# Gate and up products of an FFN by blocks: seven products of half blocks in place of eight, with the residual kept in memory

## The chip, the cores and the metric

The kernel runs on one core of a Trainium2 chip. Its time is the device time of one execution in microseconds (us). The engines are TensorE (PE, with its weight loads shown as PEld), VectorE (DVE), ScalarE (ACT), GpSimd (POOL) and SyncE (SP), which issues the DMAs.

## What is computed

Two layers, each of an FFN, a mixing sublayer and a second FFN, on x of 512 tokens by 1024 features in float32:

```
def swiglu_ffn(h, w_gu, w_down):
    a, b = jnp.split(h @ w_gu, 2, axis=-1)
    return (jax.nn.silu(a) * b) @ w_down

for l in range(DEPTH):                       # DEPTH = 2, D_FF = 2816
    h = swiglu_ffn(rmsnorm(x, ffn1_pre_g[l]), ffn1_w_gu[l], ffn1_w_down[l])
    x = x + 0.5 * rmsnorm(h, ffn1_post_g[l])
    h = mixing_sublayer(rmsnorm(x, mix_pre_g[l]), w_in[l], ...)
    x = x + rmsnorm(h, mix_post_g[l])
    h = swiglu_ffn(rmsnorm(x, ffn2_pre_g[l]), ffn2_w_gu[l], ffn2_w_down[l])
    x = x + 0.5 * rmsnorm(h, ffn2_post_g[l])
```

rmsnorm divides by the root mean square over the 1024 features and multiplies by a gain. The mixing sublayer has four branches (a gated MLP over tokens, a pooling, an attention over selected keys, a convolution of 31 taps), whose gated sum goes through w_out.

## The kernel before

Activations lie as [feature in its block of 128, block k of 8, token of 512]. Every float32 product is made of three products of halves: a rounded copy (made by ACT) and the rest (value minus copy, made by DVE or POOL). `split` does it for activations (L218 ACT, L219 DVE, or L221 and L222 with a scale), `weights` for a weight tile: a DMA of up to 512 KB into `raw` (two buffers), the copy wH on ACT (L195), the rest wL on DVE (L200, 1024 wide) or on POOL (two of 512). `mm3s` writes the matmuls (L251); each has 128 x 128 weights of its own and 512 token columns, or 256 where a sublayer's border is taken by halves of the tokens.

An FFN has 22 blocks f of 128 hidden features. For each, gate and up are products over the 8 blocks k of x: 2 x 8 x 3 = 48 matmuls of 512 columns. The operands are x times a gain per feature (xH, xL); the norm's factor by token is only applied to the results: in `gu_evac` DVE multiplies the gate product by rb_ (L453), ACT takes silu (L454), DVE multiplies with the up product (L456), and `split` makes the halves. silu is taken of the scaled gate; the scale of the up product is left to the norm behind the sublayer (`rc_prev` in `post_stats`). After each of three groups of f (GROUPS) the down product over these f is made for the 8 blocks d of the output and added up in y (L526, L528). The last four d of the last group are the tail: they are made by halves of the tokens, and the first products of the next sublayer (`head`, and `ahead` for the FFN's f = 2) lie around the norms between the two, so that PE has work while these run. The residual x stays in SBUF all the time (tiles x0 to x7).

Each engine runs its queue in the order in which the program was laid down. The chain in front of rb_ is: column sums on PE (L291), the reciprocal root on DVE in small steps (L335, L275 to L280), four diagonals (L299), their spread over the partitions on PE (L307), and ACT's copy to rb_ (L338).

Of the kernel before, what the change touches and what calls it, by code (L numbers as in the profile page):

```python
# [11 lines left out]
F32 = mybir.dt.float32  # L12
# [13 lines left out]
GROUPS = ((0, 8), (8, 15), (15, 22))  # L26
# [22 lines left out]
class Builder:  # L49
# [22 lines left out]
    def ring(self, dt=F32R):  # L72
        return self.t([P, N], dt, "h", 20)
# [41 lines left out]
    def late_consts(self):  # L115
# [7 lines left out]
        # bias of the last 256 keys of a query block: T[q, h, j] = rel_bias[bucket(q - j + 128), h]  # L123
# [5 lines left out]
        oh = self.t([P, 1024], F32, "raw", 2)  # L129
# [26 lines left out]
    def pump(self, ns):  # L156
        """emit background steps worth ns of VectorE; a step that must let products pass waits for the next call"""
# [886 lines left out]
```

## Time and profile before

| | us |
|---|---|
| median of 3 runs (2386.17 to 2389.53) | 2388.51 |
| span of the profiled execution | 2384.7 |
| PE busy | 2310.4 (97%) |
| DVE busy | 1298.2 (54%) |
| ACT busy | 820.3 (34%) |
| POOL busy | 470.8 (20%) |

The span runs from the first to the last instruction of the profiled execution; the median of the runs lies 3.8 us above it. Busy shares are means over stages that differ: in the bodies of the four FFNs, some 1220 us together, PE has no gap, DVE is busy two fifths of the time and POOL hardly at all.

### The profile page before, as it was taken

The page shows a single profiled execution, that of the slowest core. Times are in us where ns is not written, and L with a number is a line of the kernel's source. Part 1 is how long each engine was busy: PE and PEld are TensorE (multiplying, and loading weights), DVE is VectorE, ACT ScalarE, POOL GpSimd, SP SyncE. Part 2 cuts the span into 40 slices and gives each one's busy share as a digit, 9 for nine tenths or more (in the row PEclk, how much of TensorE's full clock was granted, in tenths as well). Part 3 has the DMA queues.
Part 4 walks back from the last instruction along what each step waited for, and adds up shares of the span by engine and source line. Part 5 has one row for each costly group of instructions (what it writes and reads, how often), then busy time and mean ns, then how long its engine had stood idle before and what let it go on. Part 6 is the DMA issues. An engine that isn't in the chain of part 4 may idle for free.

```text
span 2384.7 us, 28413 instructions
## 1 busy us (share of the span) xinstructions
PE 2310.4 (97%) x11158; PEld 1931.8 (81%) x11158; DVE 1298.2 (54%) x2246; ACT 820.3 (34%) x1267; POOL 470.8 (20%) x413
## 2 busy tenths in 40 slices
PE   8999998989999999999999999989899999999997
PEld 7888888767888888888888888887778888888886
DVE  5333347899734652334573333488996346524345
ACT  4232233443443432222342222344434334322221
POOL 0000003533555300000210000035445543000001
PEclk9999999999999999999999999999999999999999
DMA  5333331222223233333323333312123222332332
GB/s 167 97 105 89 111 91 61 82 65 81 83 85 98 89 91 95 96 98 95 91 80 93 108 89 105 92 60 80 62 80 98 81 90 69 107 97 94 101 93 67
DMA packets 64271, 215.69 MB, mean 90 GB/s; under 512 B 7396, under 2 KB 11144, under 8 KB 64136
## 3 DMA queue, kind: packets, MB, share of 16 engines
q1 hardware_dynamic: 64136, 213.87, 29.5%
q8 instruction: 87, 1.43, 0.3%
q14 instruction: 48, 0.39, 0.1%
HBM read 211.74 MB, written 2.10 MB: 90 GB/s over the span
## 4 chain that ended last, share of the span: by engine, by line
PE 85%; DVE 11%; issue 1%; POOL 1%; ACT 1%; DMA 0%; SPq 0%; POOLq 0%; ACTq 0%; DVEq 0%
PE mm L251 51%; PE at L251 32%; DVE ca L841 3%; DVE x L385 1%; DVE xL L396 1%; DVE t L382 1%; PE st L307 1%; DVE sc L911 1%; DVE m L910 1%; PE st L291 0%; POOL t L759 0%; DVE s L278 0%; PE at L945 0%; DVE s L280 0%; POOL wL L200 0%
## 5 line engine op out<-in xcount | busy, mean ns | idle before, releaser
L195 ACT ACTIVATE wH<-raw 128x1024 fp32r<-128x1024 f32 (+1 forms) x394 | 408.8, 1040 | 1064.6 <-issue 574.7
L251 PE MATMUL mm<-xH,wH 128*128 128x512 f32 (+1 forms) x1504 | 572.5, 390 | 8.8 <-DVE t L732 4.4
L251 PE MATMUL mm<-xH,wL 128*128 128x512 f32 (+1 forms) x1504 | 565.2, 386 | 0.0
L200 DVE TENSOR_TENSOR wL<-raw,wH 128x1024 fp32r<-128x1024 f32 (+1 forms) x292 | 349.4, 1198 | 238.8 <-ACT wH L195 238.5
L251 PE MATMUL mm<-h,wH 128*128 128x512 f32 (+1 forms) x1496 | 407.9, 353 | 0.1
L251 PE MATMUL mm<-xL,wH 128*128 128x512 f32 (+1 forms) x1504 | 393.1, 379 | 0.0
L200 POOL TENSOR_TENSOR wL<-raw,wH 128x512 fp32r<-128x512 f32 x204 | 290.3, 1446 | 351.1 <-ACT wH L195 303.8
L251 PEld LDWEIGHTS mm<-xH,wH 128*128 128x128 f32 x1504 | 284.1, 193 | 69.1 <-DVE t L732 4.9
L251 PEld LDWEIGHTS mm<-xH,wL 128*128 128x128 f32 x1504 | 284.2, 193 | 53.9 <-issue 0.9
L251 PEld LDWEIGHTS mm<-xL,wH 128*128 128x128 f32 x1504 | 278.4, 189 | 53.1
L251 PE MATMUL at<-xH,wH 128*128 128x512 f32 (+1 forms) x784 | 301.0, 385 | 7.5 <-ACT xH L221 7.4
L251 PE MATMUL at<-xH,wL 128*128 128x512 f32 (+1 forms) x784 | 297.6, 381 | 0.0
L251 PEld LDWEIGHTS mm<-h,wH 128*128 128x128 f32 x1496 | 263.2, 188 | 41.7 <-DVE t L732 0.6
L251 PE MATMUL mm<-h,wL 128*128 128x512 f32 (+1 forms) x748 | 253.8, 354 | 0.0
L251 PE MATMUL at<-h,wH 128*128 128x512 f32 (+1 forms) x776 | 219.6, 366 | 0.0
L251 PE MATMUL at<-xL,wH 128*128 128x512 f32 (+1 forms) x784 | 210.6, 378 | 0.0
L251 PEld LDWEIGHTS at<-xH,wH 128*128 128x128 f32 x784 | 149.3, 190 | 38.0 <-ACT xH L221 7.7
L189 POOL TENSOR_TENSOR h<-raw,h 128x512 fp32r<-128x512 f32 x10 | 15.1, 1534 | 807.6 <-DVE wL L200 758.3
L251 PEld LDWEIGHTS at<-xH,wL 128*128 128x128 f32 x784 | 149.0, 190 | 29.2 <-issue 1.4
L251 PEld LDWEIGHTS at<-xL,wH 128*128 128x128 f32 x784 | 147.5, 188 | 27.5
L251 PEld LDWEIGHTS at<-h,wH 128*128 128x128 f32 x776 | 140.4, 188 | 24.6
L251 PEld LDWEIGHTS mm<-h,wL 128*128 128x128 f32 x748 | 140.4, 188 | 20.4
(196 smaller groups left out, 2185.2 us busy)
## 6 DMA issues: line engine op xcount, KB each, us to landing
raw<-in_ffn_w_gu_dram SPq DMA_DIRECT2D x173, 512.0 KB, 3.6
raw<-in_w_in_dram SPq DMA_DIRECT2D x98, 512.0 KB, 3.6
raw<-in_ffn_w_down_dram SPq DMA_DIRECT2D x64, 448.0 KB, 3.4
raw<-in_ffn_w_down_dram SPq DMA_DIRECT2D x32, 512.0 KB, 3.6
raw<-in_w_branch_dram SPq DMA_DIRECT2D x16, 512.0 KB, 3.7
raw<-in_w_out_dram SPq DMA_DIRECT2D x16, 512.0 KB, 3.6
x<-in_x_dram SPq DMA_DIRECT2D x8, 256.0 KB, 6.4
out_dram<-x SPq DMA_DIRECT2D x16, 128.0 KB, 1.8
```

The source lines that it names most:

```text
L189: nc.gpsimd.tensor_tensor(lo, r, h.bitcast(F32), op=ALU.subtract)
L195: self.pin(nc.scalar.activation(h[:, :n], raw[:, :n], AF.Copy))
L200: self.pin(e.tensor_tensor(lo[:, c], raw[:, c], h.bitcast(F32)[:, c], op=ALU.subtract))
L251: self.nc.tensor.matmul(out, w[a], m[b], start=(first and i == 0), stop=(last and i == 3 * n - 1))
L307: self.nc.tensor.matmul(ps[:, s], self.ones, dg[:, s], start=True, stop=True)
L382: nc.vector.scalar_tensor_tensor(u[:, c], s.o[k][:, c], self.v(s.post[0], s.post[1] + k), pb[:, c], op0=ALU.mult, op1=ALU.mult)
L385: e.tensor_tensor(self.xt[k][:, c], self.xt[k][:, c], u[:, c], op=ALU.add)
L396: nc.vector.scalar_tensor_tensor(self.xl[k][:, c], self.xt[k][:, c], g, self.xh[k].bitcast(F32)[:, c], op0=ALU.mult, op1=ALU.subtract)
L841: nc.vector.scalar_tensor_tensor(a, hp[:, t:t + N], dw(t), a, op0=ALU.mult, op1=ALU.add)
L910: nc.vector.max(m8, sc[:, :W])
L911: nc.vector.match_replace(out=sc[:, :W], in_to_replace=m8, in_values=sc[:, :W], imm_value=GONE)
```

## The change

Of the 22 blocks f of an FFN, the first four (PLAIN) stay as they are. The other 18 are taken in nine pairs. For a pair, the weights form a 2 x 2 scheme of blocks (gate or up by the lower or upper half of the 1024 input features), and x one too (half of the features by half of the tokens, 256). A plain product of such schemes needs eight products of half blocks; the change makes it with seven, in the form of Winograd, at the price of sums of blocks before and after. Each of the seven is 2 (blocks f) x 4 (k) x 3 = 24 matmuls of 256 columns.

- `operands` makes the right sides once per FFN: x is multiplied in place by gain and rb_ (L511), then come the halves of its quarters (L520, L521) and of four sums of quarters (L530 to L533, POOL and DVE).
- `blocks` loads four weight tiles per pair, and makes four sums of them (L551, two on DVE, two on POOL) and the halves of the seven left sides (L556 ACT, L557 DVE), each two products ahead of its use.
- `units` sets the order of the products (1, 2, 6, 5, 7, 4, 3, with the next pair's 1 and 2 ahead of this pair's 4 and 3), adds the results up (ACT L632, DVE L635 to L645), takes silu and the product, and `leave` makes the halves for the down product.
- `fill` puts the finished part of the first down product (d = 0) in front of the last pair's products 4 and 3.
- As x is destroyed by `operands`, it is written to memory at the border (`x_away`) and read back when the tail's weights are loaded (`x_back`).
- The up product now carries rb_ as well, so `gu_evac` has one more multiply on POOL (L462), and `post_stats` no longer needs the factor of the norm before.
- GROUPS changes; raw has seven buffers, and one ring of 49 tiles takes in the residual and many tiles of the mixing sublayer; the convolution runs without a padded copy.

The core of the diff:

```
-GROUPS = ((0, 8), (8, 15), (15, 22))
+GROUPS = ((0, 6), (6, 14), (14, 22))
+PLAIN = 4
...
+    def x_back(self):
+        src = self.a["x"] if self.xs is None else self.xs
+        self.xt = [self.ring(F32) for _ in range(KD)]
+        for k in range(KD):
+            self.nc.sync.dma_start(self.xt[k], src[:, k, :])
...
         a1 = b.tmp()
         nc.vector.tensor_tensor(a1, pa, b.rb_, op=ALU.mult)
         nc.scalar.activation(a1, a1, AF.Silu)
+        nc.gpsimd.tensor_tensor(a1, a1, b.rb_, op=ALU.mult)
         hp = b.tmp()
         nc.vector.tensor_tensor(hp, pb, a1, op=ALU.mult)
...
+    def operands(self):
...
+        for k in range(KD):
+            nc.vector.scalar_tensor_tensor(b.xt[k], b.xt[k], b.v(self.pre[0], self.pre[1] + k), b.rb_,
+                                           op0=ALU.mult, op1=ALU.mult)
...
+        def halves(parts):
+            h, l = b.ring(), b.ring()
+            for i, src in enumerate(parts):
+                w = src.shape[-1]
+                d = slice(i * w, (i + 1) * w)
+                nc.scalar.activation(h[:, d], src, AF.Copy)
+                nc.vector.tensor_tensor(l[:, d], src, h.bitcast(F32)[:, d], op=ALU.subtract)
+            return [(h[:, c], l[:, c]) for c in (lo, hi)]
+        for p in range(H):
+            op[1][p], op[2][p] = halves([b.xt[p][:, lo], b.xt[p + H][:, lo]])
+        yield
+        for p in range(H):
+            b11, b12, b21, b22 = b.xt[p][:, lo], b.xt[p][:, hi], b.xt[p + H][:, lo], b.xt[p + H][:, hi]
+            s13, s24 = b.tmp(), b.tmp()
+            nc.gpsimd.tensor_tensor(s13[:, lo], b12, b11, op=ALU.subtract)
+            nc.vector.tensor_tensor(s24[:, lo], b22, s13[:, lo], op=ALU.subtract)
+            nc.gpsimd.tensor_tensor(s13[:, hi], b22, b12, op=ALU.subtract)
+            nc.gpsimd.tensor_tensor(s24[:, hi], b21, s24[:, lo], op=ALU.subtract)
+            op[6][p], op[4][p] = halves([s24])
+            op[5][p], op[7][p] = halves([s13])
...
+        def one():
+            r = halves(a11)
+            tt(nc.vector, S1, a21, a22, ALU.add)
+            return r
+        def two():
+            r = halves(a12)
+            tt(nc.gpsimd, a21, a11, a21, ALU.subtract)
+            tt(nc.vector, a11, S1, a11, ALU.subtract)
+            return r
+        def six():
+            r = halves(a11)
+            tt(nc.gpsimd, a12, a12, a11, ALU.subtract)
+            return r
+        return {1: one, 2: two, 6: six, 5: lambda: halves(S1), 7: lambda: halves(a21), 4: lambda: halves(a22),
+                3: lambda: halves(a12)}
...
+    def product(self, i, out, w, fresh):
+        for c in range(2):
+            o = out[:, c * 256:(c + 1) * 256]
+            todo = []
+            for p in range(KD // 2):
+                ws = slice(c * N + p * P, c * N + (p + 1) * P)
+                h, l = self.op[i][p]
+                todo += [(w[0][:, ws], h), (w[1][:, ws], h), (w[0][:, ws], l)]
...
+        order = [(f, i) for f in fs for i in (1, 2, 6, 5, 7, 4, 3)]
+        for n in range(len(fs) - 1):
+            at = 7 * n + 5
+            order[at:at + 4] = order[at + 2:at + 4] + order[at:at + 2]
...
+            if i in (1, 6, 7):
+                s[f"t{i}"] = b.tmp()
+                nc.scalar.activation(s[f"t{i}"], bank, AF.Copy)
+            if i == 2:
+                g = s["g0"] = s["t1"]
+                nc.vector.tensor_tensor(g, bank, g, op=ALU.add)
+                nc.scalar.activation(g, g, AF.Silu)
+            if i == 7:
+                nc.vector.tensor_tensor(s["t7"], s["Z"], s["t7"], op=ALU.add)
+            if i == 4:
+                nc.vector.tensor_tensor(s["g0"], bank, s["g0"], op=ALU.mult)
+                out[f] = [(b.ring(), b.ring()) for _ in range(2)]
+                self.leave(out[f], s["g0"], 0)
+            if i == 3:
+                g = s["t6"]
+                nc.vector.tensor_tensor(g, bank, g, op=ALU.add)
+                nc.scalar.activation(g, g, AF.Silu)
+                nc.gpsimd.tensor_tensor(g, g, s["t7"], op=ALU.mult)
+                self.leave(out[f], g, 1)
```

Three places show what now stands in the queues. All are in the second FFN of the first layer. On VectorE of the kernel before, behind the chain to rb_ (the L299 diagonals), there come the weights' lower halves (wL) and, for each f, three steps on products that lie in PSUM (at, mm) or on their result (h):

```order
L299 TENSOR_SCALAR t_9636<-ident,rc_9615 128x128 x4
L351 TENSOR_TENSOR s_2223_11871<-rc_9615 128x2
L200 TENSOR_TENSOR wL_9736<-raw_9733,wH_9735 128x1024
L453 TENSOR_TENSOR t_9700<-at_9286,rb__1841_9616 128x512
L200 TENSOR_TENSOR wL_9801<-raw_9798,wH_9800 128x1024
L456 TENSOR_TENSOR t_9703<-at_9287,t_9700 128x512
L453 TENSOR_TENSOR t_9709<-mm_9288,rb__1841_9616 128x512
L219 TENSOR_TENSOR h_9706<-t_9703,h_9705 128x512
```

Now, some 30 instructions behind the same diagonals, the operands' sums (L531, of t tiles that POOL writes) and lower halves (L521) stand in the same queue; h_11868 is the last one that product 6 needs, h_11872 the last one of product 5:

```order
L531 TENSOR_TENSOR t_11862<-h_10919,t_11861 128x256
L521 TENSOR_TENSOR h_11830<-t_11819,h_11829 128x512
L460 TENSOR_TENSOR t_11887<-at_11749,rb__2026_11611 128x512
L521 TENSOR_TENSOR h_11840<-t_11834,h_11839 128x512
L557 TENSOR_TENSOR wL_11981<-raw_11899,wH_11980 128x1024
L521 TENSOR_TENSOR h_11844<-t_11833,h_11843 128x512
L464 TENSOR_TENSOR t_11891<-at_11750,t_11887 128x512
L521 TENSOR_TENSOR h_11854<-t_11848,h_11853 128x512
L635 TENSOR_TENSOR t_11947<-mm_11953,t_11947 128x512
L521 TENSOR_TENSOR h_11858<-t_11847,h_11857 128x512
L557 TENSOR_TENSOR wL_12011<-raw_11903,wH_12010 128x1024
L521 TENSOR_TENSOR h_11868<-t_11862,h_11867 128x512
```

So the queue that had a few steps per f behind rb_ now has the whole making of the operands between rb_ and products 6 and 5.

On GpSimd the kernel before has nothing between the last residual sums of the border (L385) and the end of that FFN but one mask for the next layer's use (L585):

```order
L385 TENSOR_TENSOR x_62<-x_62,t_9425 128x256
L385 TENSOR_TENSOR x_64<-x_64,t_9449 128x256
L385 TENSOR_TENSOR x_66<-x_66,t_9473 128x256
L385 TENSOR_TENSOR x_68<-x_68,t_9485 128x256
L585 AFFINE_SELECT raw_10346<-raw_10346 128x512
```

After the change the same queue has these instead, in this order: a weight sum, multiplies by rb_ (L462), a second weight sum, and twelve sums of x's quarters:

```order
L390 TENSOR_TENSOR h_10919<-h_10919,t_11479 128x256
L551 TENSOR_TENSOR raw_11899<-raw_11897,raw_11899 128x1024
L462 TENSOR_TENSOR t_11695<-t_11695,rb__2026_11611 128x512
L462 TENSOR_TENSOR t_11799<-t_11799,rb__2026_11611 128x512
L551 TENSOR_TENSOR raw_11901<-raw_11901,raw_11897 128x1024
L462 TENSOR_TENSOR t_11809<-t_11809,rb__2026_11611 128x512
L530 TENSOR_TENSOR t_11819<-h_10912 128x256
L532 TENSOR_TENSOR t_11819<-h_10916,h_10912 128x256
L530 TENSOR_TENSOR t_11833<-h_10913 128x256
L532 TENSOR_TENSOR t_11833<-h_10917,h_10913 128x256
L530 TENSOR_TENSOR t_11847<-h_10914 128x256
L533 TENSOR_TENSOR t_11820<-h_10916,t_11820 128x256
```

The sums stand behind the second and third multiply, each of which waits for a silu.

On PE the kernel before goes straight on with matmuls of 512 columns, one f behind the other:

```order
L251 MATMUL at_9642<-xH_9196,wL_9646 128x512
L251 MATMUL at_9642<-xH_9197,wH_9645 128x512
L251 MATMUL at_9642<-xH_9197,wL_9646 128x512
L251 MATMUL at_9642<-xH_9198,wH_9645 128x512
L251 MATMUL at_9642<-xH_9198,wL_9646 128x512
```

Now product 2 (mm_11953) is followed by products 5 (mm_12014) and 6 (mm_11922), which alternate as their operands (h) are written; the stretch shown lies 14 matmuls behind the end of product 2:

```order
L594 MATMUL mm_11922<-h_11854,wH_11917 128x256
L594 MATMUL mm_12014<-h_11857,wH_11949 128x256
L594 MATMUL mm_12014<-h_11857,wL_11950 128x256
L594 MATMUL mm_11922<-h_11867,wH_11917 128x256
L594 MATMUL mm_11922<-h_11867,wL_11918 128x256
L594 MATMUL mm_12014<-h_11858,wH_11949 128x256
L594 MATMUL mm_12014<-h_11871,wH_11949 128x256
L594 MATMUL mm_11922<-h_11868,wH_11917 128x256
L594 MATMUL mm_11922<-h_11825,wH_11917 128x256
```

So PE's first products of a pair stand directly behind the operands' last halves, with no other product between.

## Rows read from the trace of the kernel before

**Rows 1.** The page's head, the busy shares, and the chain's shares by engine.
```profile
span 2384.7 us, 28413 instructions
...
PE 2310.4 (97%) x11158; PEld 1931.8 (81%) x11158; DVE 1298.2 (54%) x2246; ACT 820.3 (34%) x1267; POOL 470.8 (20%) x413
...
PE 85%; DVE 11%; issue 1%; POOL 1%; ACT 1%; DMA 0%; SPq 0%; POOLq 0%; ACTq 0%; DVEq 0%
```
**Rows 2.** Busy time by stretch: an FFN, a border, another FFN.
```profile
core 0: us, PE busy (x) PEld busy (x) DVE busy (x) ACT busy (x) POOL busy (x), PEclk, DMA share, GB/s
...
39.80:346.30 306.50, 306.50 (x1344) 251.54 (x1343) 119.14 (x135) 90.51 (x116) 1.13 (x3) 1.00 0.33 98
346.30:430.00 83.70, 77.71 (x510) 70.59 (x509) 64.92 (x140) 35.80 (x67) 28.96 (x27) 0.98 0.26 76
852.30:1156.20 303.90, 303.90 (x1338) 250.83 (x1337) 118.77 (x133) 88.54 (x113) 0.00 (x0) 1.00 0.32 98
```
**Rows 3.** Chain in order of time: start, us, what (512-column matmuls).
```profile
204.01 16.32 PE at L251 x72
```
**Rows 4.** Timeline, PE, 256-column matmuls of a tail: start, us, what.
```profile
355.89 0.28 PE L251 MATMUL mm<-h,wL 128*128 128x256 f32 x1
...
357.07 0.28 PE L251 MATMUL mm<-h,wL 128*128 128x256 f32 x1
```
**Rows 5.** Timeline, PE, DVE and ACT, from the column sums to rb_.
```profile
844.47 0.95 PE L291 MATMUL st<-ones,t 128*128 128x1 f32 x8
...
846.34 1.22 DVE L200 TENSOR_TENSOR wL<-raw,wH 128x1024 fp32r<-128x1024 f32 x1
...
847.56 1.22 DVE L200 TENSOR_TENSOR wL<-raw,wH 128x1024 fp32r<-128x1024 f32 x1
...
851.31 1.02 PE L307 MATMUL st<-t,ones 128*128 128x512 f32 x2
...
852.36 0.60 ACT L338 ACTIVATE rb__1337_6876<-st 128x512 f32<-128x512 f32 x1
```
**Rows 6.** Groups by line and shape: count, busy us, mean ns, idle before.
```profile
L200 DVE TENSOR_TENSOR wL<-raw,wH 128x1024 fp32r<-128x1024 f32 x228 | 279.5, 1227 | 217.8 <-ACT wH L195 217.5
L219 DVE TENSOR_TENSOR h<-t,h 128x512 fp32r<-128x512 f32 x106 | 74.8, 707 | 3.6 <-ACT h L218 2.8
L222 DVE SCALAR_TENSOR_TENSOR xL<-x,vec,xH 128x512 fp32r<-128x512 f32 x8 | 5.6, 746 | 0.0
L437 DVE TENSOR_TENSOR t<-t,t 128x256 f32<-128x256 f32 x65 | 28.1, 432 | 22.6 <-ACT t L435 19.8
L528 DVE TENSOR_TENSOR y<-mm,y 128x512 f32<-128x512 f32 x28 | 19.4, 691 | 61.7 <-PE mm L251 61.7
L744 POOL TENSOR_TENSOR y<-y,t 128x512 f32<-128x512 f32 x32 | 41.4, 1295 | 40.3 <-DVE t L742 35.8 <-DVE s L864 4.5
L437 POOL TENSOR_TENSOR t<-t,t 128x256 f32<-128x256 f32 x53 | 41.2, 778 | 403.7 <-ACT t L435 401.4
L526 ACT ACTIVATE y<-at 128x512 f32<-128x512 f32 x16 | 9.6, 597 | 59.9 <-PE at L251 59.9
L454 ACT ACTIVATE t<-t 128x512 f32<-128x512 f32 x88 | 54.3, 617 | 0.1
L307 PEld LDWEIGHTS st<-t,ones 128*128 128x128 f32 x44 | 7.4, 199 | 20.0 <-DVE t L299 16.1 <-issue 3.5
```
**Rows 7.** Timeline, DVE, one operation behind the other in an FFN.
```profile
1229.31 1.23 DVE L200 TENSOR_TENSOR wL<-raw,wH 128x1024 fp32r<-128x1024 f32 x1 [1.50 <-ACT wH L195]
1230.45 0.69 DVE L453 TENSOR_TENSOR t<-at,rb__1841_9616 128x512 f32<-128x512 f32 x1
...
1233.90 0.69 DVE L219 TENSOR_TENSOR h<-t,h 128x512 fp32r<-128x512 f32 x1
1234.51 0.68 DVE L456 TENSOR_TENSOR t<-mm,t 128x512 f32<-128x512 f32 x1
```
**Rows 8.** Timeline, DVE, seven 256-wide operations while POOL is idle.
```profile
400.68 2.85 DVE L396 SCALAR_TENSOR_TENSOR xL<-x,vec,xH 128x256 fp32r<-128x256 f32 x7
```
**Rows 9.** Timeline, the same line of DVE beside operations of POOL.
```profile
819.48 4.38 DVE L396 SCALAR_TENSOR_TENSOR xL<-x,vec,xH 128x256 fp32r<-128x256 f32 x6
...
820.22 5.87 POOL L437 TENSOR_TENSOR t<-t,t 128x256 f32<-128x256 f32 x7 [1.62 <-ACT t L435]
```
**Rows 10.** Busy time and granted clock (PEclk) in three stretches of a border.
```profile
378.00:384.20 6.20, 4.09 (x32) 3.66 (x31) 6.20 (x14) 4.34 (x9) 4.13 (x4) 1.00 0.37 103
384.20:387.60 3.40, 3.40 (x18) 3.40 (x18) 3.40 (x7) 3.40 (x10) 2.60 (x4) 0.50 0.30 120
```
**Rows 11.** DMA issues: tile, operation, count, KB each, us to landing.
```profile
raw<-in_ffn_w_gu_dram SPq DMA_DIRECT2D x173, 512.0 KB, 3.6
...
x<-in_x_dram SPq DMA_DIRECT2D x8, 256.0 KB, 6.4
```

More of the change, by code (lines that the diff above doesn't have):

```diff
@@ L86, in consts @@
         nc, sb, a = self.nc, self.sb, self.a
-        self.xt = [sb.tile([P, N], F32, name=f"x{k}") for k in range(KD)]
+        self.xs = None
         self.vec = sb.tile([P, DEPTH * NV], F32, name="vec")
@@ L315, in new_x @@
     def new_x(self):
[L316 to L317 removed]
+        self.xh = [self.ring() for _ in range(KD)]
+        self.xl = [self.ring() for _ in range(KD)]
     @property
@@ L390, in post_steps @@
                 nc.scalar.activation(self.xh[k][:, c], self.xt[k][:, c], AF.Copy, scale=g)
+                if not first:
+                    self.x_away(k)
             yield 600
@@ new lines, in product @@
+    def product(self, i, out, w, fresh):
+        b = self.b
+        for c in range(2):
[5 more added lines that the diff above has]
+                todo += [(w[0][:, ws], h), (w[1][:, ws], h), (w[0][:, ws], l)]
+            for n, (x, m) in enumerate(todo):
+                b.run_due()
+                b.pe += 118
+                b.nc.tensor.matmul(o, x, m, start=(fresh and c == 0 and n == 0), stop=(n == len(todo) - 1),
+                                   skip_group_check=True)
@@ L503, in rest @@
             nxt = b.subs[min(b.subs.index(self) + 1, len(b.subs) - 1)]
-            if gi == 1 and isinstance(nxt, Mix):
-                nxt.params()
+            last = gi == len(GROUPS) - 1
             hm = []
-            for f in range(f0, f1):
-                if f < 3:
-                    pa, pb = self.hp[f]
-                else:
+            if gi == 0:
+                hm.append(self.gu_evac(*self.hp[0]))
+                ops = self.operands()
+                next(ops)
+                for f in range(3, PLAIN):
                     wa, wb = self.gu_weights(f)
@@ L514, in rest, with fill @@
                     b.gemm(pb, wb, b.xm)
-                hm.append(self.gu_evac(pa, pb))
+                    self.hp.append([pa, pb])
+                hm.append(self.gu_evac(*self.hp[1]))
+                hm.append(self.gu_evac(*self.hp[2]))
+                for _ in ops:
+                    pass
+                for f in range(3, PLAIN):
+                    hm.append(self.gu_evac(*self.hp[f]))
+            part = []
+            def fill(done):
+                done = hm + done
+                w, p = self.dn_weights(0, f0, f1), b.cyc()
+                b.mm3(p, b.pairs(w, done, FULL), True, False)
+                part.extend([w, p, len(done)])
+            hm = hm + self.units(range(max(f0, PLAIN), f1, 2), fill)
+            if last and isinstance(nxt, Mix):
+                nxt.params()
             self.hm, self.g = hm, (f0, f1)
-            last = gi == len(GROUPS) - 1
             if last:
@@ L533, in tail_weights @@
         b = self.b
+        b.x_back()
         ds = range(KD - TAIL, KD)
```

149 lines of the change are left out of this document (103 added, 46 removed).

## The prediction, made before the result was known

> **What bounds the kernel now.** I began with busy shares and the chain [rows 1]: TensorE (PE) is busy 97% of 2384.7 us and carries 85% of the chain, VectorE (DVE) 11%. Then the stretches [rows 2]: in the body of an FFN PE is busy all of 303.9 us (1338 matmuls, 0.227 us each) while DVE is busy 119 us, ScalarE (ACT) 89 and GpSimd (POOL) nothing; the idle time of PE lies at the borders between sublayers (77.7 of 83.7 us in one). So in an FFN the count of matmul columns sets the time, DVE has 60% to spare, and whoever takes columns away and loads the vector engines instead wins only as long as these stay hidden.
>
> **The gain on PE.** By the program, 3504 matmuls of 512 columns go and 6144 of 256 columns come (36 pairs of f, each 96 of 512 replaced by 168 of 256; 48 more become halves since the tail's group now has eight f's). A 512-column step is 16.32/72 = 0.2267 us [rows 3]; 256-column steps stand (357.07−355.89)/10 = 0.118 us apart, each with weights of its own [rows 4]. Gain: 3504 × 0.2267 − 6144 × 0.118 = 794.4 − 725.0 = 69, or 71 with the 0.2271 of the whole stretch; the last digit of the ten short steps leaves 6 to either side. I take **70**. Seven eighths of the columns are worth only 9% since the short step costs 52% of the long one.
>
> The Trainium skill (TensorE: Matmul & The Clock Gate, Back-to-back issue gap) gives an isolated gap of N/2.4 + 2.5 ns, so 216 and 109 ns; by that the gain would be an estimated 85 us. The trace differs by its own spacings above, which decide.
>
> **What the vector engines do in its place, per FFN.** (a) The operands of the seven products, once the factor rb_ is known; (b) the steady pairs; (c) the ends of groups; (d) the norm chain before rb_.
>
> Durations: two operands in SBUF on DVE, 1024 wide 1.22 us, 512 wide 0.71 (with a vector factor 0.75), 256 wide 0.43; from PSUM 0.69; on POOL 512 wide 1.30, 256 wide 0.78; ACT copy 0.60, silu 0.62 [rows 6]. In a row each begins some 0.08 us before the last ends: 1.14 after the 1024-wide op, 0.61 after a 512-wide one [rows 7], 0.40 for 256 wide with a factor [rows 8]. I use these spacings: 1.14, 0.60, 0.66 (with factor), 0.34; from PSUM 0.61 to 0.65, taken 0.65; POOL 1.25 and 0.70. A 1024-wide POOL op isn't in the trace: from 256 to 512 columns POOL's op grows by 0.52 us, so 2.3 (1.30 + 2 × 0.52) is my estimate, between 1.25 and 2.6.
>
> DVE and POOL get in each other's way. Alone, seven 256-wide DVE ops take 2.85 us [rows 8]. Beside POOL ops, six of the same line take 4.38 us (0.73 each), and seven POOL ops 5.87 (0.84 each) [rows 9]. Alone the thirteen would take 6 × 0.40 + 7 × 0.70 = 7.3 us; together they took 826.09 − 819.48 = 6.6. Almost nothing overlaps: 0.9 of the sum. DVE ops that read PSUM keep their 0.69 [rows 6], so these can lie beside POOL.
>
> The Trainium skill (SBUF — State Buffer, SBUF: two separate sides) says why: a DVE op with two SBUF inputs and a GpSimd op that reads SBUF lock one port pair for a whole instruction. The 4.38 and 5.87 us agree at 256 columns; no run here shows a 1024-wide POOL op.
>
> **(a) Operands**, counted from T0, when rb_ is there (ACT's 852.36 + 0.60 in the second FFN [rows 5]). From the spread at 851.31 [rows 5] PE still has 64 products of 512 (14.5 us) and reaches product 1 at T0 + 13.2; products 1 and 2 (48 × 0.118 = 5.7) last to 18.9; products 5 and 6 could end at 24.5. DVE's queue from T0: L460 0.65, two scalings, then L464, which must wait for silu (0.62) and POOL's new multiply (1.25): done at 4.2. Six more scalings (4.0), L232 (0.6), six of L521 (2.0): 10.8. L460, L557 and two L521 end at 13.3, just in time for product 1. POOL stood still, as its second multiply (in order, ahead of all sums) waits for that L460 and its silu: it starts at 12.1. From there POOL has 1.25 + 2.3 + 1.25 + 12 × 0.70 = 13.2 us of work. DVE's ops with two SBUF inputs until the last half that products 6 and 5 need: 2 × 0.34 + 4 × 1.14 + 2 × 0.6 + 4 × 0.34 + 8 × 0.6 = 12.6. Behind one another 25.8, at 0.9 of it 23.2: ready at 12.1 + 23.2 = 35.3. If nothing overlaps and DVE's six PSUM ops (3.9) stand in line as well: 41.8. I take the middle, 38.5. Behind the last half 27 of the 48 matmuls are left (3.2 us; the order has 6, 9, 2, 2, 2 ahead of it). PE stands 38.5 + 3.2 − 24.5 = 17.2 us per FFN (14.0 to 20.5). In the first FFN PE has 1.6 us more to do. Sum 4 × 17.2 − 1.6 = **67** (54 to 80).
>
> Such waits cost clock: at one border, behind 6.2 us in which PE worked only 4.1, it had 3.4 us at 0.50 of the clock (1.2 for 2.4 GHz) [rows 10], worth 1.7 us. Four times 2 us: **8** (7 to 14).
>
> **(b) Steady pairs.** PE needs 168 × 0.118 = 19.8 us per pair (before 21.8). DVE: seven lower halves and two sums, 9 × 1.14 = 10.3, two of 256 0.7, four PSUM ops 2.6. POOL: two sums 4.6, one multiply 1.25, two of 256 1.4: 7.3. Port work 10.3 + 0.7 + 7.3 = 18.3 us, at 0.9 of it 16.5; all in line with the PSUM ops 20.9. That is 83 to 105% of PE's time, where before DVE had 39%. The 24 passages from pair to pair should cost 0 to 1.5 us each, 0.4 by the lower end: **10** (0 to 36). The 512 KB loads (3.6 us to landing [rows 11]) are as many bytes as before and start early enough (98 GB/s in these stretches [rows 2], now a tenth more).
>
> **(c) Ends of groups.** Before product 3's results reach the down product, L645 0.65, silu 0.62, POOL 1.30, ACT's and DVE's halves some 0.8 pass: 3.4 to 3.9 us. In front of them stand 12 matmuls of d=1, 2.7 us. Before, this edge cost under 0.5 us. 12 ends × 0.7: **8** (0 to 25).
>
> **(d) Norm chain.** Between PE's column sums (844.47) and the spread, DVE had two 1024-wide ops in the chain [rows 5]; now four, and POOL's a21 beside them: 2.3 us longer. The spread now stands some seven matmuls (1.6 us) later. Three FFNs × 1: **3** (0 to 9).
>
> Beside these, the residual's 40 loads and 40 writes (256 KB each; x took 6.4 us to land [rows 11]) lie in stretches where DMA is a quarter to a third busy [rows 2] and are loaded a tail ahead of their use: 0 (−5 to +10, the shorter norm after the FFN and the longer tail being the minus).
>
> **Sum:** −70 + 67 + 8 + 10 + 8 + 3 = +26. Span 2384.7 + 26 = 2410.7; the median stands 3.8 above the span (2388.5 against 2384.7), so **2414.5 us**, 1.1% slower. The saved columns are spent while PE waits for the operands they need.
>
> **Rivals.** *Operands hidden, faster.* If DVE and POOL do not exclude each other here (other widths, other ops than in rows 9), the halves are ready when DVE's own 12.6 + 3.9 us are done: 12.1 + 16.5 = 28.6, stall 7.3 per FFN, in all 28, clock 7, pairs and ends 10: −70 + 45 = −25, 2364 us. It decides from a stall of about 11 us per FFN downwards. For it: DVE's 60% idle time. Against: rows 8 and 9.
> *Balance.* All at their low ends, 54 + 7 + 9: −70 + 70 = 0, 2388.5 us.
> *The port binds everywhere.* Stall 80, clock 14, pairs 36, ends 15, chain 9: −70 + 154 = +84, 2472 us. For it: 20.9 us in line against 19.8 per pair. Against: PSUM ops aren't slowed.
> *The saving isn't there,* should 256-column matmuls with new weights each time be held by weight loads, which last 0.19 us [rows 6]: +440 us. The spacing of 0.118 with a new weight each [rows 4] speaks against it; 1 in 100.
>
> **How the numbers follow.** Forecast (2395 to 2445) 0.55, hidden 0.20, balance 0.10, port everywhere 0.14, no saving 0.01. The range: half of the hidden case lies above 2365, most of the last but one below 2468: 2366 to 2468. Within 0.2% is 2383.7 to 2393.3, about what a measurement can tell from no change: faster 0.20, same 0.10, slower 0.70.
>
> **What would show it.** Per FFN one block of PE idle some 20 us after rb_, of 14 to 20 us in pieces, which ends with DVE's L521 or POOL's L533, with the granted clock at 0.5 behind it; in that stretch DVE's 512-wide subtractions at 1 us or more while POOL runs; DVE over 70% busy in the pairs, PE gapless there but for under a microsecond; 3504 and 6144 matmuls at 0.227 and 0.118. If PE idles under 8 us there, step (a) was wrong; if POOL and DVE overlap at their lone durations, its 0.9 was; if PE waits in each pair for L557, step (b) was.

## The result, and the profile after

The changed kernel takes 2439.87 us (median of 4 runs, 2439.63 to 2443.67), the kernel before 2387.82 us in the same series: a ratio of 1.0222, 95% interval 1.0208 to 1.0237. It is 2.2% slower. The forecast was slower by 1.1%, 2414.5 us, in a range of 2366 to 2468.

The page of the kernel after: the span, the busy shares, and the chain's shares by engine.

```profile
span 2437.9 us, 35144 instructions
...
PE 2277.7 (93%) x13798; PEld 2027.2 (83%) x13798; DVE 1683.2 (69%) x2538; ACT 1024.6 (42%) x1635; POOL 893.1 (37%) x653
...
PE 69%; DVE 17%; issue 7%; POOL 4%; ACT 2%; DMA 1%; SPq 0%; POOLq 0%; DVEq 0%; ACTq 0%
```

Beside [rows 1], TensorE (PE) is busy for 33 us less and idle for 86 us more; VectorE (DVE) and GpSimd (POOL) have taken on 385 and 422 us.

Where the 53 us of span went is seen from one landmark that every sublayer has, the start of ACT's copy to rb_ (L338 before, L351 after). Two of its rows in the timeline of the kernel after, at the two ends of the first mixing sublayer (start us, us, engine, line, operation):

```profile
426.96 0.60 ACT L351 ACTIVATE rb__658_4051<-st 128x512 f32<-128x512 f32 x1 [5.58 <-PE st L320]
...
878.68 0.60 ACT L351 ACTIVATE rb__1435_7882<-st 128x512 f32<-128x512 f32 x1 [4.97 <-PE st L320]
```

The differences of these starts, in us, for the two kernels and for four of the experiments below:

| from rb_ to rb_ | before | after | plain_all | mix_in_ring | front6 | cover_and_ring |
|---|---|---|---|---|---|---|
| start to the first | 39.8 | 43.7 | 43.0 | 43.2 | 42.7 | 42.8 |
| FFN 1, layer 1 | 377.7 | 383.3 | 375.5 | 375.5 | 372.7 | 365.5 |
| mixing, layer 1 | 434.8 | 451.7 | 447.6 | 436.8 | 447.0 | 436.7 |
| FFN 2, layer 1 | 376.8 | 381.5 | 372.6 | 372.6 | 369.6 | 361.1 |
| FFN 1, layer 2 | 374.8 | 378.1 | 374.1 | 372.5 | 370.8 | 362.6 |
| mixing, layer 2 | 430.9 | 445.4 | 444.2 | 433.6 | 441.8 | 434.4 |
| FFN 2, layer 2, to the end | 349.8 | 354.2 | 348.8 | 348.8 | 347.0 | 337.5 |

So of +53 us the four FFNs, where the products by blocks are, took +18; the two mixing sublayers, whose arithmetic the change doesn't touch, took +31; the start took +4. The FFN's part is the one that the prediction worked out, and its largest term can be read directly. PE behind the first pair's product 2, in the second FFN (rb_ is there at 1260.77), with what ended each wait in brackets:

```profile
1281.22 0.28 PE L594 MATMUL mm<-h,wH 128*128 128x256 f32 x1
1286.60 0.58 PE L594 MATMUL mm<-h,wH 128*128 128x256 f32 x1 [5.11 <-ACT h L520]
...
1290.66 0.79 PE L594 MATMUL mm<-h,wH 128*128 128x256 f32 x2 [3.26 <-DVE h L521]
...
1294.67 0.79 PE L594 MATMUL mm<-h,wH 128*128 128x256 f32 x2 [3.01 <-DVE h L521]
...
1298.81 0.80 PE L594 MATMUL mm<-h,wH 128*128 128x256 f32 x2 [0.36 <-DVE h L521]
```

Four waits, all for the operands' halves (L520, L521). DVE's last two of these, and the granted clock in a part of the stretch (PE busy, PEld, DVE, ACT, POOL, then PEclk):

```profile
1260.17 0.60 ACT L351 ACTIVATE rb__2026_11611<-st 128x512 f32<-128x512 f32 x1 [4.58 <-PE st L320]
...
1298.08 1.28 DVE L521 TENSOR_TENSOR h<-t,h 128x512 fp32r<-128x512 f32 x2
```
```profile
1288.00:1291.40 3.40, 0.74 (x3) 0.71 (x3) 2.86 (x4) 0.79 (x3) 3.19 (x4) 0.50 0.00 0
...
1294.80:1298.00 3.20, 3.20 (x15) 3.20 (x16) 3.20 (x5) 1.55 (x4) 0.00 (x0) 0.50 0.18 71
```

The last half is done at 1299.36, that is rb_ + 38.6 us; the prediction had 38.5. PE came to product 1 at rb_ + 14.8, and product 7, 96 short matmuls later, begins at rb_ + 41.8: 15.5 us more than 96 × 0.12. In the four FFNs this loss, waits and half clock together, is 16.9, 15.4, 15.5 and 16.4 us: 64 us.

### The profile page after: what moved, and what is told of

Same layout as the page of the kernel before. It is cut to its first block, busy times and chain, and to the rows that moved or that the text cites. A ratio compares the mean times of both kernels' runs of the same rounds, so it can differ in the third digit from the quotient of the medians.

```text
span 2437.9 us, 35144 instructions
## 1 busy us (share of the span) xinstructions
PE 2277.7 (93%) x13798; PEld 2027.2 (83%) x13798; DVE 1683.2 (69%) x2538; ACT 1024.6 (42%) x1635; POOL 893.1 (37%) x653
## 4 chain that ended last, share of the span: by engine, by line
PE 69%; DVE 17%; issue 7%; POOL 4%; ACT 2%; DMA 1%; SPq 0%; POOLq 0%; DVEq 0%; ACTq 0%
PE mm L264 30%; PE at L264 13%; PE mm L594 12%; PE at L594 12%; DVE raw L1026 3%; DVE h L1096 1%; DVE h L390 1%; DVE m L1095 1%; DVE h L403 1%; POOL t L462 1%; POOL t L647 1%; DMA raw<-in_ffn_w_gu_dram 1%; DVE wL L557 1%; PE st L320 1%; POOL t L530 1%
## 5 line engine op out<-in xcount | busy, mean ns | idle before, releaser
L264 PE MATMUL mm<-h,wH 128*128 128x512 f32 (+1 forms) x3280 | 939.6, 367 | 17.8 <-ACT wH L212 6.4
L264 PEld LDWEIGHTS mm<-h,wH 128*128 128x128 f32 x3280 | 597.2, 192 | 121.9 <-ACT wH L212 8.9
L264 PE MATMUL mm<-h,wL 128*128 128x512 f32 (+1 forms) x1640 | 577.9, 368 | 1.1 <-POOL wL L217 1.1
L594 PE MATMUL mm<-h,wH 128*128 128x256 f32 x2240 | 430.6, 288 | 50.1 <-DVE h L521 27.0
L557 DVE TENSOR_TENSOR wL<-raw,wH 128x1024 fp32r<-128x1024 f32 x252 | 381.7, 1527 | 100.8 <-ACT wH L556 97.8
L594 PEld LDWEIGHTS mm<-h,wH 128*128 128x128 f32 x2240 | 363.3, 196 | 55.3 <-DVE h L521 30.3
L264 PE MATMUL at<-h,wH 128*128 128x512 f32 (+1 forms) x1296 | 383.0, 367 | 21.0 <-ACT h L234 11.7
L551 POOL TENSOR_TENSOR raw<-raw,raw 128x1024 f32<-128x1024 f32 x72 | 198.5, 2757 | 476.1 <-DVE raw L551 234.4
L264 PEld LDWEIGHTS mm<-h,wL 128*128 128x128 f32 x1640 | 311.5, 194 | 49.9 <-POOL wL L217 2.1
L556 ACT ACTIVATE wH<-raw 128x1024 fp32r<-128x1024 f32 x252 | 263.9, 1053 | 188.1 <-PE at L264 58.0
L594 PE MATMUL at<-h,wH 128*128 128x256 f32 x1792 | 336.4, 283 | 0.5 <-ACT t L632 0.5
L594 PE MATMUL mm<-h,wL 128*128 128x256 f32 x1120 | 320.7, 286 | 0.0
L264 PEld LDWEIGHTS at<-h,wH 128*128 128x128 f32 x1296 | 241.5, 192 | 63.4 <-ACT h L656 12.7
L594 PEld LDWEIGHTS at<-h,wH 128*128 128x128 f32 x1792 | 285.5, 192 | 1.6 <-ACT t L632 0.7
L594 PEld LDWEIGHTS mm<-h,wL 128*128 128x128 f32 x1120 | 219.2, 196 | 0.8 <-issue 0.2
```

What stands on the lines that cost most here:

```text
L264: self.nc.tensor.matmul(out, w[a], m[b], start=(first and i == 0), stop=(last and i == 3 * n - 1))
L551: tt = lambda e, o, x, y, op: e.tensor_tensor(o, x, y, op=op)
L556: nc.scalar.activation(h, src, AF.Copy)
L557: nc.vector.tensor_tensor(l, src, h.bitcast(F32), op=ALU.subtract)
L594: b.nc.tensor.matmul(o, x, m, start=(fresh and c == 0 and n == 0), stop=(n == len(todo) - 1), skip_group_check=True)
```

## The experiments

**Blocks or storage?** plain_all keeps the change's storage and leaves out its products by blocks.

```diff
-            if gi == 0:
-                hm.append(self.gu_evac(*self.hp[0]))
-                ops = self.operands()
...
-            hm = hm + self.units(range(max(f0, PLAIN), f1, 2), fill)
+            for f in range(f0, f1):
+                if f < 3:
+                    pa, pb = self.hp[f]
+                else:
+                    wa, wb = self.gu_weights(f)
...
+                hm.append(self.gu_evac(pa, pb))
```

> All 22 blocks f of every FFN stay plain (no products by blocks, no operands); the storage of the change stays: the residual written away and read back, one ring, raw with seven buffers, the mixing sublayer's tiles in them, the extra multiply on POOL. Storage theory (the two mixing sublayers got 12 us longer each before their last norm because of where their tiles and weights now lie): the FFNs are back at the times of the kernel before, the mixing sublayers stay at 445 to 452 us from rb_ to rb_, in all 2388 + 20 to 30 = 2408 to 2418 us. Rival, block theory (the mixing sublayers suffer from what the FFN by blocks leaves in the queues): 2384 to 2394 us.

Measured: 2403.94 us, ratio to before 1.0059 (1.0044 to 1.0074). The storage theory holds in its place: the mixing sublayers stay at 447.6 and 444.2 us. The FFNs are not just back but 1 to 4 us shorter than before (table), so the total is 4 us under what was expected. With the storage as it is, the products by blocks cost 2440 − 2404 = 36 us.

**Why the mixing sublayers?** In the timelines, DVE computes the attention's scores; before, two of its 384-wide steps took 1.34 us, and POOL made its last weight halves ahead of them:

```profile
434.94 2.70 POOL L200 TENSOR_TENSOR wL<-raw,wH 128x512 fp32r<-128x512 f32 x2 [2.75 <-ACT wH L195]
```
```profile
441.03 1.34 DVE L897 SCALAR_TENSOR_TENSOR sc<-t,wi,sc 128x384 f32<-128x384 f32 x2
```

After the change the same two steps take 2.90 us, and a 128-wide one 1.26 in place of 0.28, since POOL makes its weight halves just then:

```profile
450.46 2.82 POOL L217 TENSOR_TENSOR wL<-raw,wH 128x512 fp32r<-128x512 f32 x2 [41.48 <-PE at L264]
453.92 3.00 POOL L217 TENSOR_TENSOR wL<-raw,wH 128x512 fp32r<-128x512 f32 x2 [0.64 <-ACT wH L212]
```
```profile
450.79 2.90 DVE L1082 SCALAR_TENSOR_TENSOR h<-t,wi,h 128x384 f32<-128x384 f32 x2 [0.25 <-ACT t L1077]
...
454.52 1.26 DVE L1083 TENSOR_TENSOR h<-h,cmask 128x128 f32<-128x128 f32 x1
```

POOL had been idle for 41 us: in ACT's queue the weight copies that it needs now stand between and behind the scores' copies, where before they stood ahead of them. The four long-lived tiles that the change puts in raw (two of attention values, the convolution's input and its sum) are the suspects. vv_ring takes the first two out:

```diff
-            both = b.rawt(F32R)
-            h, lo = both[:, 0:N], both[:, N:2 * N]
-            b.split(pv, h, lo)
+            h, lo = b.split(pv)
```

> The changed kernel with one edit: in the mixing sublayer the halves of the attention values lie in the ring and no longer in raw. Theory: these two raw buffers held the next weight columns back, so that their lower halves came on POOL beside the attention's score chain on VectorE, and the two waits of PE there grew from 3.6 and 5.1 to 8.1 and 8.1 us. With the edit the weight copies stand ahead of the scores again: the mixing sublayers lose 8 to 12 us each, 2416 to 2424 us. Rival (the score chain is late for another reason, such as the residual's transfers): 2436 to 2442 us.

Measured: 2431.83 us, ratio to before 1.0173 (1.0158 to 1.0188). A gain of 8 us in all, where 8 to 12 us for each of the two mixing sublayers was expected: the first comes to 443.8 us, the second stays at 445.0. In the first, PE's two waits on the attention were 3.4 and 4.9 us before and are 6.7 and 7.9 us after the change (the expectation has 8.1 for both); here they are 4.9 and 7.8 us, so the second one didn't shrink. Two of the tiles are a part of the cause and not all of it. mix_in_ring takes all four out (vv_ring's edit and the one below), in the plain kernel so that nothing else moves; mix_in_ring_raw2 also goes back to two raw buffers.

```diff
-        both = b.rawt()
...
-            hc = both[:, j * N:(j + 1) * N]
+            hc = b.ring(F32)
...
-        ca = b.rawt()
         for j in range(2):
-            a = ca[:, j * N:(j + 1) * N]
+            a = b.ring(F32)
```

> All blocks f plain as in plain_all (2404 us), and the mixing sublayer's tiles (attention values, convolution's input and sum) in the ring, none in raw. Theory A (those four long-lived tiles in raw move the weight loads and with them the order of the queues): both mixing sublayers fall from 447.6 and 444.2 to about 435, 2404 - 20 = 2384 us (2380 to 2390). Rival B (seven raw buffers let the weights come early, whatever lies in them, and shift POOL's and VectorE's work against the scores): less than a third of it, 2397 to 2404 us.

> As mix_in_ring, with two raw buffers as in the kernel before in place of seven. Theory A: no difference to mix_in_ring beyond 3 us. Rival B: the mixing sublayers come back only here, 2380 to 2388 us while mix_in_ring stays at 2397 or above; the start (43 us before the first rb_, 39.8 in the kernel before) comes back to 40 in either theory if early weight loads hold x up.

Measured: mix_in_ring 2386.46 us, ratio to before 0.9991 (0.9982 to 1.0001), 17.5 us under plain_all; the mixing sublayers are back to within 2 and 3 us of the kernel before:

```profile
418.65 0.60 ACT L351 ACTIVATE rb__577_3114<-st 128x512 f32<-128x512 f32 x1 [0.82 <-PE st L320]
...
855.48 0.60 ACT L351 ACTIVATE rb__1358_6949<-st 128x512 f32<-128x512 f32 x1 [0.82 <-PE st L320]
```

The four tiles are the cause, and seven raw buffers by themselves are not. The order is back as well: POOL is done with its weight halves at 438.63, before all but the first of the scores' steps (438.36), as in the kernel before.

```profile
436.11 2.52 POOL L217 TENSOR_TENSOR wL<-raw,wH 128x512 fp32r<-128x512 f32 x2 [2.90 <-ACT wH L212]
```

With two buffers the mixing sublayers are as good (436.4 and 433.9 us) but the whole takes 2405.04 us: the first FFNs of both layers, those ahead of a mixing sublayer, grow by 10 us each. There PE waits for a weight of the last down products:

```profile
341.40 0.80 PE L264 MATMUL at<-h,wH 128*128 128x512 f32 x1 [7.85 <-ACT wH L212]
```

That sublayer's small parameters pass through raw just ahead of those weights, which is the likely reason; it wasn't tried by itself. So theory A's "no difference" was wrong for this side, and the start didn't come back to 40 us either (42.9); what makes it 3 us later wasn't tried. Since mix_in_ring keeps the residual in memory and equals the kernel before, this storage costs nothing in sum, given seven raw buffers. It does so by a balance (table): the start is 3 us longer, the two mixing sublayers 5, the four FFNs 10 shorter. What the residual's 80 transfers cost by themselves was not separated.

**What makes the operands late?** no_sums leaves the sixteen sums out.

```diff
-            s13, s24 = b.tmp(), b.tmp()
-            nc.gpsimd.tensor_tensor(s13[:, lo], b12, b11, op=ALU.subtract)
...
+            s13, s24 = b.xt[p], b.xt[p + H]
```

> The changed kernel without the sixteen sums of x's quarters per FFN (twelve on POOL, four on VectorE): the halves are made of quarters of x instead, so that this part of the computation is left out. Theory of the shared port: POOL and VectorE work behind one another, the last half comes 0.9 x (12 x 0.70 + 4 x 0.34) = 8.8 us earlier per FFN, PE's wait of 13 us shrinks to about 4, and the half clock behind it goes in part: 35 to 45 us in all, 2395 to 2405 us. Rival (VectorE's own queue sets the time, POOL's sums lie beside it): only the four sums on VectorE count, 6 us in all, 2430 to 2436 us.

Measured: 2416.23 us, 24 us faster, between the two. PE's loss per FFN, counted as above, falls from 16.9, 15.4, 15.5 and 16.4 to 10.7, 11.0, 8.7 and 11.0 us, by 23 in all. The sums on POOL matter (the rival had 6 us), but only two thirds of the 35 us that the theory had comes back; where the other third went wasn't followed up. Two edits that move work between the engines, with none left out, tell more. sums_on_dve moves POOL's twelve sums to DVE, onto the queue that PE waits for:

```diff
-            nc.gpsimd.tensor_tensor(s13[:, lo], b12, b11, op=ALU.subtract)
+            nc.vector.tensor_tensor(s13[:, lo], b12, b11, op=ALU.subtract)
...
-            nc.gpsimd.tensor_tensor(s13[:, hi], b22, b12, op=ALU.subtract)
-            nc.gpsimd.tensor_tensor(s24[:, hi], b21, s24[:, lo], op=ALU.subtract)
+            nc.vector.tensor_tensor(s13[:, hi], b22, b12, op=ALU.subtract)
+            nc.vector.tensor_tensor(s24[:, hi], b21, s24[:, lo], op=ALU.subtract)
```

> The changed kernel with the twelve sums of x's quarters per FFN on VectorE in place of POOL. Theory of the shared port (the two engines work behind one another): 12 x 0.70 us on POOL become 12 x 0.34 on VectorE, the last half comes about 3.5 us earlier, 10 to 16 us faster in all, 2424 to 2430 us. Rival (POOL's sums lie beside VectorE's queue, which alone sets the end): VectorE's queue grows by 4.1 us per FFN, 2450 to 2458 us.

Measured: 2427.80 us, ratio to before 1.0157 (1.0140 to 1.0174), 12 us faster than the change, as the shared port has it, though DVE now has twelve instructions more. From rb_ (1253.29 + 0.60) to the end of the last half it is 34.7 us, 3.9 less than in the kernel after:

```profile
1287.31 0.69 DVE L464 TENSOR_TENSOR t<-at,t 128x512 f32<-128x512 f32 x1 [1.18 <-POOL t L462]
1287.92 0.68 DVE L521 TENSOR_TENSOR h<-t,h 128x512 fp32r<-128x512 f32 x1
```

The durations in the timelines say why. In the kernel after, 11 of DVE's 45 steps between rb_ and the last half take longer than the same step beside an idle POOL, by 7.3 us in all; here 2 of 54 do, by 2.1 us. DVE's own queue up to that point grew by the sums (4.1 us) and lost two weight halves and one step on a product (2.9 us), which now stand behind it; by its own work alone the end would have come 1.2 us later.

mult_on_dve frees POOL's queue of the multiplies that wait for silu:

```diff
-        nc.gpsimd.tensor_tensor(a1, a1, b.rb_, op=ALU.mult)
         hp = b.tmp()
-        nc.vector.tensor_tensor(hp, pb, a1, op=ALU.mult)
+        nc.vector.tensor_tensor(hp, pb, b.rb_, op=ALU.mult)
+        nc.vector.tensor_tensor(hp, hp, a1, op=ALU.mult)
```

> The changed kernel with the up product's multiply by rb_ on VectorE (from PSUM, ahead of silu, then one more product in SBUF) in place of POOL's multiply behind silu: POOL's sums no longer stand behind two multiplies that wait for silu. Theory of the shared port: what counts is the sum of work, POOL loses 3.8 us, VectorE gains about as much (0.6 each from PSUM and from SBUF, four times, less the two waits of 1.2 us for POOL): the last half comes 2 to 4 us earlier, 2424 to 2434 us. Rival (the order counts: the sums wait in POOL's queue for silu): they start some 8 us earlier and so does the end, 2405 to 2415 us.

Measured: 2435.38 us, 4.5 us faster. In the timeline of mult_on_dve, POOL's first and sixth sum, and DVE's last half:

```profile
1259.24 1.03 POOL L530 TENSOR_TENSOR t<-h 128x256 f32<-128x256 f32 x1 [5.81 <-DVE h L511]
...
1275.63 4.75 POOL L533 TENSOR_TENSOR t<-h,t 128x256 f32<-128x256 f32 x2 [6.91 <-DVE t L531]
```
```profile
1295.32 0.68 DVE L521 TENSOR_TENSOR h<-t,h 128x512 fp32r<-128x512 f32 x1
```

With rb_ there at 1256.98, the first sum begins 2.3 us behind it in place of 18.6, and the last half still ends at 39.0 us (38.6). But only five of the twelve sums gain this head start. The sixth waits for a sum of DVE (L531), which stands in DVE's queue behind the plain f's steps, and begins 18.7 us behind rb_. PE's loss falls all the same, from 64 to 57 us in the four FFNs; by what wasn't followed up. So the run did not test what it was made for: for most of the sums the order stayed, held by DVE's queue in place of POOL's. Both forecasts missed, the port theory's (the last half 2 to 4 us earlier, 2424 to 2434 us) by little, the rival's (2405 to 2415) by far. That the port, and not the order, sets this end rests on sums_on_dve and the durations; an order in which all twelve sums start early wasn't tried.

**Can the latency be hidden?** front6 keeps six f plain, which is the whole first group, so that two more f and eight down products stand between rb_ and the first pair.

```diff
-PLAIN = 4
+PLAIN = 6
...
-            hm = hm + self.units(range(max(f0, PLAIN), f1, 2), fill)
+            if f1 > PLAIN:
+                hm = hm + self.units(range(max(f0, PLAIN), f1, 2), fill)
```

> The changed kernel with six plain blocks f ahead of the pairs, that is the whole first group, and this group's down products between the operands and the first pair (8 pairs per FFN instead of 9). Theory: the wait for operands is one latency of some 15 us after which the pairs keep up; 54 us of matmuls more in front of it hide it wholly. It gives back 61 us of waits and half clock and one group's end per FFN (4 x 1.4), and costs 4 pairs x 2 us: 2440 - 58 = 2382 us (2376 to 2390). Rival (VectorE and POOL stay behind for long, so that the wait moves into the first pairs or the down products): half of it or less, 2405 to 2440 us.

Measured: 2394.35 us (10 runs), ratio to before 1.0027 (1.0015 to 1.0038): 45.5 us of the expected 58. The pairs don't wait for operands any more, and the kernel comes to within 0.3% of the kernel before. A new wait stands in each FFN, in front of the first down products (4.8 to 5.0 us, some 20 us in all, more than the 12.5 that are missing):

```profile
1275.88 0.79 PE L264 MATMUL at<-h,wH 128*128 128x512 f32 x1 [5.03 <-ACT h L231]
```

These need the last plain f's halves, and DVE evacuates that f behind the whole making of the operands.

**The ends of groups.** In the kernel after, PE and POOL at one end:

```profile
1432.51 0.39 PE L264 MATMUL mm<-h,wL 128*128 128x512 f32 x1
1434.18 0.50 PE L264 MATMUL at<-h,wH 128*128 128x512 f32 x1 [1.29 <-ACT h L656]
```
```profile
1431.89 1.79 POOL L647 TENSOR_TENSOR t<-t,t 128x512 f32<-128x512 f32 x1 [0.97 <-ACT t L646]
```

At each of twelve ends PE's next start comes 1.2 to 1.45 us later than one step of 0.227 us (of this, 1.0 to 1.3 us is idle time in the profile). fill_two puts more in front:

```diff
                     w, p, n = part
+                    w1, p1 = self.dn_weights(1, f0, f1), b.cyc()
+                    b.mm3(p1, b.pairs(w1, hm, FULL)[:n], True, False)
                     b.mm3(p, b.pairs(w, hm, FULL)[n:], False, True)
+                elif d == 1 and part:
+                    p = p1
+                    b.mm3(p1, b.pairs(w1, hm, FULL)[n:], False, True)
```

> The changed kernel with more cover at the ends of groups: the finished part of the second down product (18 matmuls of 512 columns in the last two groups, 12 in the first) is put between product 3 of the last pair and the last operands, 4.1 us in place of 2.7. Theory: the chain from product 3 (sum, silu, POOL's multiply, halves) is 3.9 us, so that the twelve waits of 1.2 to 1.45 us go in the last two groups and shrink little in the first: 8 x 1.4 = 11 us to 16 us faster, 2424 to 2430 us. Rival (the chain starts later, as VectorE or POOL has other work in front of it, or PE is caught up elsewhere): under 4 us, 2436 us or more.

Measured: 2429.09 us, 10.8 us faster. The same end in windows of 10 us, first of the kernel after, then of fill_two:

```profile
1428.00:1438.00 10.00, 8.71 (x47) 7.16 (x47) 5.58 (x7) 4.34 (x8) 3.96 (x3) 1.00 0.30 105
```
```profile
1422.00:1432.00 10.00, 10.00 (x53) 8.25 (x53) 5.57 (x7) 5.02 (x9) 3.98 (x3) 1.00 0.34 105
```

**All of it.** cover_and_ring is front6 with the sums of the operands put behind the evacuation of the plain f, fill_two's cover, and the mixing sublayer's tiles in the ring.

```diff
                 hm.append(self.gu_evac(*self.hp[2]))
-                for _ in ops:
-                    pass
...
+                    hm.append(self.gu_evac(pa, pb))
+                for _ in ops:
+                    pass
```

> All mends in one: six plain f and the first group's down products in front of the first pair, the sums for the operands put behind the evacuation of the plain f (in front6 the down products waited 5.2 us per FFN for those), the longer cover at the ends of groups, the mixing sublayer's tiles in the ring. From the changed kernel's 2440: front6 -45.5, its waits -20, ends 8 x 1.4 = -11, mixing sublayers -15 to -20: 2344 to 2352 us, faster than both kernels. If pairs are bound by VectorE and POOL once nothing else delays them, or the down products wait again: 2365 to 2380 us.

Measured: 2340.26 us (2338.68 to 2342.31), ratio to before 0.9794 (0.9779 to 0.9808): 2.1% faster than the kernel before, 4.1% faster than the change, and 4 us under what was expected. An FFN from rb_ to rb_, first in the kernel after, then here:

```profile
1260.17:1638.29 378.12, 358.20 (x2442) 333.24 (x2442) 260.96 (x332) 166.87 (x259) 127.16 (x83) 0.97 0.31 103
```
```profile
1206.00:1568.60 362.60, 356.01 (x2375) 328.59 (x2374) 256.85 (x329) 163.35 (x252) 123.34 (x82) 1.00 0.34 110
```

PE's idle time falls from 20 to 6.6 us and the granted clock is 1.00 in place of 0.97 of full speed, with one pair fewer by blocks.

## Why the prediction was right, and where its size was off

The direction was right, and so were the cause and the place of its largest term; the forecast of +26 us was half of the measured +53 of span, and some 20 of these 53 lie where the prediction put nothing. Term by term:

- **Gain on PE:** 70 foreseen, 57 measured. The counts were right; the spacing of the short matmuls was not. In the pairs of the kernel after, the chain has 48 of them in 5.76 us, 0.120 us each, where [rows 4] gave 0.118 for a tail. Over 6048 of them that is 12 us, twice the 6 us that the prediction allowed for the row's last digit.

```profile
1362.69 5.76 PE at L594 x48
1368.45 5.76 PE mm L594 x48
```

  The row was read rightly: the median of some 2000 such steps in the tails of the kernel before is 0.118 us. It is the tails' own steps that stand 0.120 apart once the storage has changed, here in the chain of the kernel before and of the kernel after; in plain_all, which has no products by blocks, they do too. So the longer step doesn't belong to the products by blocks; what makes it longer stays open.

```profile
363.35 2.47 PE at L251 x21
```
```profile
363.91 8.63 PE mm L264 x72
```

- **Operands:** 67 + 8 foreseen, 64 measured with the clock. The mechanism held: the last half at 38.6 us for 38.5, and the port as its reason (sums_on_dve and the durations there). That it came within 0.1 us is luck, since 38.5 was the middle between 35.3 and 41.8. Two parts were mis-sized. PE came to product 1 later than foreseen (14.8 for 13.2 us), so it stood idle for 11.7 to 13.4 us per FFN, less than the 14 to 20 us named as the sign. And the 8 us for the clock did not come on top: by the prediction's own sum without them product 7 begins at 38.5 + 3.2 = 41.7 us, measured 41.8, as the half clock fell in the time in which PE would have waited for the last halves anyway. That DVE's steps on PSUM keep their 0.69 us beside POOL could not be read from [rows 6], as POOL is idle during every one of the steps that its row on L528 counts; the kernel after shows it, inside the POOL sum that began at 1274.81 and took 2.39 us:

```profile
1274.88 0.69 DVE L464 TENSOR_TENSOR t<-mm,t 128x512 f32<-128x512 f32 x1 [1.19 <-POOL t L462]
```

- **Pairs:** 10 foreseen, 0 measured. PE has no gap from pair to pair (one of 0.5 us in all the passages), while DVE is busy 84% of the time, here in one stretch:

```profile
1362.69:1414.50 51.81, 51.81 (x434) 51.81 (x434) 43.73 (x38) 28.54 (x41) 23.18 (x13) 1.00 0.38 123
```

  The mean durations on the profile's page (1.53 us for DVE's weight half, 1.22 in [rows 6]; 2.76 for POOL's sum) say that the port is shared here as well; the weights' halves, made two products ahead, are there in time all the same.

```profile
L557 DVE TENSOR_TENSOR wL<-raw,wH 128x1024 fp32r<-128x1024 f32 x252 | 381.7, 1527 | 100.8 <-ACT wH L556 97.8
...
L551 POOL TENSOR_TENSOR raw<-raw,raw 128x1024 f32<-128x1024 f32 x72 | 198.5, 2757 | 476.1 <-DVE raw L551 234.4
```

- **Ends of groups:** 8 foreseen, about 16 measured (12 × 1.2 to 1.45): POOL's multiply took 1.79 us beside DVE's weight half where 1.30 alone was put in.
- **Norm chain before rb_:** 3 foreseen, about 10 measured. PE waits 2.2 us for the diagonals at each of three places, and does its next matmuls at half clock (0.50), so that each place costs some 3.3 us:

```profile
1258.46 1.67 PE L320 MATMUL st<-t,ones 128*128 128x512 f32 x2 [2.21 <-DVE t L312]
```
```profile
1260.20:1262.00 1.80, 1.80 (x5) 1.40 (x5) 1.80 (x3) 1.04 (x2) 0.00 (x0) 0.50 0.00 0
```

- **"Beside these ... 0 (−5 to +10)": the step that failed.** It looked at the residual's transfers and at the borders, and put nothing down for the mixing sublayers, whose arithmetic stays but whose tiles the change moves. Measured: the start +4, the borders behind the FFNs about −8 (what the FFNs of plain_all gained), the inside of the mixing sublayers +24 (31 less the norm chain at their ends), in all +20, beyond the bounds given. plain_all and mix_in_ring show that the moved tiles did it; that they did it by the order of ACT's and POOL's queues, so that the POOL halves came to lie beside the scores, is read from the timelines of the first mixing sublayer and not tried by itself. The order of the queues in these sublayers could have been compared before the result was known.

With the measured terms, −57 + 64 + 16 + 10 + 20 = +53. That these close so well owes something to rounding: the norm chain's 10 is read from three places, and the borders' −8 is taken over from plain_all.

Of the rivals, "operands hidden" is refuted in the form it had (no exclusion between DVE and POOL), and "the port binds everywhere" holds for the operands and not for the pairs. The upper part of the range was needed, but for a reason that none of the cases held; that the result still lies in it is to this extent luck. (The 0.19 us of a weight load, on which the rival without a saving rests, is not the row that [rows 6] shows, 199 ns; the rival fails either way.)

## What to carry to other kernels

A saving on the bound engine has a latency to pay for its new operands: count the work of the engines that share a port as one queue, and put that much independent work of the bound engine between the factor that they need and their first use. Here that, the longer cover at the ends and one pair fewer turned a loss of 36 us for the blocks into a gain of 46 (mix_in_ring's 2386 to 2340); front6, with the work in front alone, is 45.5 us faster than the change. And tiles that change their buffer pool change the order of queues far away: compare the queues of every stage, also of those whose arithmetic stays as it was.

## What the runs showed of the hardware beyond expectation

In the rows looked at, of 256, 512 and 1024 columns, DVE operations on two SBUF operands and POOL operations excluded one another. While POOL's 1024-wide sum and the 512-wide multiply ran (2.39 and 2.28 us), DVE's two operations took 2.20 and 1.79 us in place of 1.2 and 0.7:

```profile
1274.81 2.39 POOL L551 TENSOR_TENSOR raw<-raw,raw 128x1024 f32<-128x1024 f32 x1
1277.16 2.28 POOL L462 TENSOR_TENSOR t<-t,rb__2026_11611 128x512 f32<-128x512 f32 x1
```
```profile
1276.08 2.20 DVE L557 TENSOR_TENSOR wL<-raw,wH 128x1024 fp32r<-128x1024 f32 x1
1278.21 1.79 DVE L232 TENSOR_TENSOR h<-t,h 128x512 fp32r<-128x512 f32 x1
```

This is what the Trainium skill (SBUF — State Buffer, SBUF: two separate sides) says of a lock held for a whole instruction, now also seen for a 1024-wide POOL operation. And behind waits of PE of 5.1 and 3.3 us with a few matmuls between, the granted clock was 0.50, the lower of its two levels (1.2 GHz), for about 10 us (1288 to 1298), so that even matmuls whose operands were there stood 0.21 us apart in place of 0.12 (15 in 3.2 us).
